# A fetched row's second operand moved to PSUM, with a new order of the pass over the experts

## The chip, the core and the metric

The kernel runs on one NeuronCore of a Trainium2 chip. Its engines run side by side, each through its own queue in order: PE (TensorE, matrix products), DVE (VectorE), ACT (ScalarE), POOL (GpSimd), and SP, which here only issues DMA transfers. Data lies in HBM, in SBUF (128 partitions) and in PSUM, 8 banks of 512 float32 per partition, into which PE writes its products. The metric is device microseconds (us) of one execution, lower is better.

## What is computed

One block of a diffusion backbone over 1024 tokens of width 1024: a state-space scan and long convolutions side by side, an output projection, and then PEER: per token 8 heads choose 16 experts each out of 16384, an expert being a row of `peer_u` and a row of `peer_v`. Only this last part is changed:

```python
def block(hb):
    q = (hb @ wq).reshape(PEER_BLOCK, PEER_HEADS, 2, PEER_DKEY // 2)
    s = jnp.einsum('thsd,snd->thsn', q, subkeys).astype(jnp.float32)
    s1, i1 = lax.top_k(s[:, :, 0], PEER_TOPK)
    s2, i2 = lax.top_k(s[:, :, 1], PEER_TOPK)
    ...
    idx = e1 * PEER_KEYS + e2
    gate = jax.nn.softmax(sc, axis=-1).astype(hb.dtype)
    u_sel = u_tab[idx]
    v_sel = v_tab[idx]
    act = jax.nn.gelu(jnp.einsum('td,thkd->thk', hb, u_sel), approximate=False) * gate
    return jnp.einsum('thk,thkd->td', act, v_sel)
```

Then follow the residual `h + g2 * peer` and a last RMS norm.

## The kernel before

The 1024 tokens are 8 blocks of 128, treated in two ways at the same time.

**Dense tokens**, blocks 0 to 4 (ND = 5, 640 tokens): their products with all 16384 experts, in 128 tiles of 128 experts, are made on PE, and the gates (zero where an expert isn't chosen) are multiplied in. Every float32 factor is split into a high part (ACT, a copy) and a low part (a subtraction on DVE or POOL), and a product is three matmuls: high by high, high by low, low by high.

- `score` (L1650): gelu of the dense tokens' products with a tile of `peer_u`. Tile `x_raw` is loaded (512 KB), split into `x_uh`, `x_ul`; 48 matmuls (8 x 3 x two halves of 320 tokens, L1665) go to `x_s`, two PSUM banks (SN = 2); one Gelu of 640 on ACT makes `x_a` (L1668).
- `up` (L1671): takes `x_a`, from `score` or, for tiles 0 to 47 (NE = 48), from memory (`d_A`), where they were put ahead of time; multiplies the gates `x_g` (DVE, L1684) and splits the result into `x_ah`, `x_al` (AB = 5 buffers each).
- `load_v` (L1631): half a tile of `peer_v`, 128 x 512, 256 KB; `x_vr` (VR = 2 raw buffers) is split into `x_vh` (ACT, L1638) and `x_vl` (POOL, L1639), VB = 4 buffers; `ahead_v` keeps VA = 3 ready.
- `down` (L1698): 15 matmuls (5 blocks x 3, L1712) of one A tile and one V tile into five PSUM banks `x_acc` at once (6 buffers); after the fourth tile of a group (SC = 4), DVE adds the five banks to the output `x_o` (L1719).

**The other three blocks**: `gathered` (L1563) fetches for each token its 128 rows of `peer_u` and 128 of `peer_v`, by indirect DMA from POOL's queue (L1556): one instruction fetches one row for each of 128 tokens, 512 KB, into one of the `rows` buffers (8 in the pass, 4 before it). For `peer_u`, DVE multiplies the fetched tile by the block's own rows `e_f` and sums (L1572); for `peer_v`, DVE adds it times a weight to an accumulator, also a tile named `e_f` (L1583). Both `e_f` lie in SBUF and share one buffer (EF = 1). 3 x 256 = 768 such tiles are fetched. `finish` (L1587) ends a block.

**The order.** `peer` (L1779) finds the chosen experts (`Route`) and spreads the gates; beside this run the first fetched rows and the 48 tiles computed ahead. Then `run` (L1754) passes over the 128 tiles in 32 groups of four: the first half of a group's output, tile by tile, then the up steps of the next group between the down steps of the second half, with `share` fetched rows after each step. Groups 0 to 11 hold the tiles computed ahead, groups 12 to 31 compute theirs. `last_half` ends the pass. A gather isn't put ahead of the last POOL split (`pace`). The order of each engine's queue is written out before the run by a scheduler that works from the program's order, what is ready, and buffers; it may put a later matmul ahead of one that would wait.

Of the kernel before, what the change touches and what calls it, by code (L numbers as in the profile page):

```python
# [21 lines left out]
D = 1024  # L22
# [9 lines left out]
class Kern:  # L32
# [11 lines left out]
    def pool(self, name, bufs=1, right=False, **kw):  # L44
        """a pool whose tiles wait for what stood on their own bytes alone"""
        return self.tc.tile_pool(name=name, bufs=bufs, side="right" if right else "left", reuse_waits="tile", **kw)

    def split(self, src, hi, lo, pool=False):
        """hi + lo == src, both exact in the tensor engine's one-pass float32."""
        self.nc.scalar.activation(hi, src, AF.Copy)  # L50
        (self.nc.gpsimd if pool else self.nc.vector).tensor_sub(lo, src, hi.bitcast(F32))  # L51

    def rstd(self, pool, ssum, n, shape, name):
        """1 / sqrt(ssum / n + eps)"""
# [7 lines left out]
    # ---------------------------------------------------------------- modulation  # L62
# [15 lines left out]
    def mod_sum(self, wp, s, j):  # L78
        """256 columns of the modulation for x (j = 0) or the context (j = 1), to be summed over the partitions"""
# [13 lines left out]
    def mod_norm1(self, ps, wp, j):  # L93
        """shift and scale of the first norm, features on the partitions, by 256 features"""
# [16 lines left out]
    def mod_rows(self, wp):  # L111
        """g1, sh2, norm2 * (1 + sc2), g2 as rows, to memory"""
# [18 lines left out]
    def row(self, pool, j, name):  # L131
        """row j of rows on all partitions"""
# [10 lines left out]
    # ---------------------------------------------------------------- x -> xT  # L143
# [5 lines left out]
    def normalize(self, wk, xs, xns, sq):  # L149
        """rows over their root mean square"""  # L150
# [8 lines left out]
    def xT(self, ps, wk, xns, b0, j, ks=range(8)):  # L159
        """transposes, modulates and splits blocks of tokens of x (j = 0) or the context (j = 1)"""  # L160
# [12 lines left out]
    # ---------------------------------------------------------------- in-projection  # L173
    def step(self, n):
        """goes on with the work beside"""
# [17 lines left out]
    def mm3_feat(self, outs, hi, lo, ks=range(8)):  # L193
        """outs: [(psum, 1 for the context, token offset, n)]; out[f, t] = sum_d w[d, f] x[t, d]"""
# [11 lines left out]
    def first_slab(self, ps, wp, wk, xs, mod, slab):  # L206
        """modulates x and takes it through the first slab's products as the modulation comes in"""
# [17 lines left out]
    def conv(self, acc, p, n, w, b, taps):  # L225
        """acc[:, t] = b + sum_j w[j] p[:, t + j - taps // 2], zero outside"""
# [11 lines left out]
    def to_tokens(self, ps, stage, acc, n):  # L238
        """stage[t, block, f] = acc[f, block * 128 + t]"""
# [96 lines left out]
    def softplus(self, x, tmp):  # L336
        """max(x, 0) + log1p(exp(-|x|)); log1p(e) = 2 atanh(e / (2 + e)); tmp: three scratches"""
# [92 lines left out]
class Ssd:  # L430
    """bidirectional chunked state-space scan; the context's states are carried in"""
# [65 lines left out]
    def advance(self, new, old, x, b, c, d):  # L497
        """new = old * exp(total) + sum_s B[s] (x w)[s]"""
# [17 lines left out]
    def states(self):  # L516
        """the states left of each chunk in the backward direction, to memory; the first forward state"""
# [36 lines left out]
    def load_cum(self, n):  # L554
        """the running sums of four heads, both directions, on all partitions"""
# [7 lines left out]
    def run(self):  # L563
        """all chunks, by groups of four heads: the first steps of a group go along with the last of the one before"""
# [25 lines left out]
    def first(self, c, g, loaded):  # L590
        """the weights between the tokens of a chunk before C B, and the inputs times their steps"""
# [31 lines left out]
    def second(self, c, g, loaded, made):  # L623
        """what a group of heads gives"""
# [28 lines left out]
    def done(self, c, loaded):  # L653
        """the state goes on; the chunk's output, normalized"""
# [18 lines left out]
class Hyena:  # L673
    """Long convolutions as products with DFT matrices, 2048 points for 1024 tokens.

    t = 128 n1 + n2 and k = k1 + 16 k2: a butterfly over n1 (on the vector engines) leaves the real and
    imaginary parts of k1 = 0..8, and a matrix over n2 for each k1 (on the tensor engine) gives the
    spectrum. Pair 0 holds the real sequences k1 = 0 and k1 = 8; the frequency 1024 takes the place of
    the imaginary part of frequency 0. The way back is the transpose. The work goes by slabs of W
    channels."""  # L680
# [13 lines left out]
    def tiles(self, p):  # L694
        """the four matrices of a pair: (out 0 of in 0, out 0 of in 1, out 1 of in 0, out 1 of in 1)"""
# [8 lines left out]
    def sin(self, x, r):  # L704
        """sin(x) in place, reduced to [-pi, pi] first"""
# [13 lines left out]
    def mlp(self):  # L719
        """the hidden layers of the filters' network; the last one's high parts, and below them its low parts"""  # L720
# [33 lines left out]
    def butterfly(self, u):  # L754
        """yields A = (real part, minus the imaginary part) of the sums over n1, pair by pair"""
# [122 lines left out]
    def filters(self):  # L878
        """the spectra of the two-sided filters (the biases with them), to memory"""
# [69 lines left out]
    def colmajor(self, dst, src, q):  # L949
        """dst[(w r), block] = rows of src in the grid's column-major order"""  # L950
# [359 lines left out]
ND = 5  # L1310
# [646 lines left out]
```

## Time and profile before

| | us |
|---|---|
| median of 3 runs | 4568.08 (4556.21 to 4576.03) |
| profiled execution, first to last instruction (its span) | 4564.0 |
| first fetched row's DVE instruction | 1994 |
| first matmul of a down step | 2774.6 |
| last instruction that computes (x_o, L1610) begins | 4552.3 |

A row of the profile's groups reads: line, engine, operation, output and inputs by the program's names, shapes, count | time in which at least one was running, mean of one in ns | idle time of the engine just before them, and who ended it. A row of a view of waits: who waited, for whom, total us, times, longest. A row of the windows view gives a stretch and the busy time of each engine in it with the count of instructions, then the granted PE clock, the busy share of the DMA engines and what they moved.

### The profile page before, as it was taken

The numbers are of one execution on the slowest core, as the hardware profiler recorded it, in microseconds if no ns is written. First come the engines' busy times: TensorE is split into PE (matmuls) and PEld (weight loads), VectorE is DVE, ScalarE is ACT, GpSimd is POOL, SyncE is SP. The second block draws the span as 40 slices with busy tenths as digits, with TensorE's granted clock in tenths as the row PEclk, the third lists the DMA queues.
The fourth block names the chain that finished last, engine by engine and source line by source line (L and its number), as shares of the span: only waits on it lengthen the run. The fifth ranks groups of instructions, "written<-read, shape, count | busy, mean of one in ns | idle before, by whom it ended". The sixth has DMA issues, their size and how long they took to land. (4 is left out here: it accounts for less than half of the span.)

```text
span 4564.0 us, 60591 instructions
## 1 busy us (share of the span) xinstructions
PE 3884.8 (85%) x21449; PEld 3372.0 (74%) x21449; DVE 3808.3 (83%) x6917; ACT 1325.5 (29%) x2292; POOL 2849.2 (62%) x2155
## 2 busy tenths in 40 slices
PE   5998998997876986888898877777989999998896
PEld 4776776786765875687898876655878888787784
DVE  5766888557999896699999995888798888888898
ACT  3323332234342221232225673111212222222221
POOL 2333434447777563065539895676787877788786
PEclk8999999998888998899999998889999999999998
DMA  6332333567644446456536447888798888888987
GB/s 202 99 114 99 111 124 107 162 200 232 192 159 137 145 135 178 157 209 237 185 139 212 170 164 267 290 294 290 263 314 309 303 308 307 273 299 295 317 298 242
DMA packets 509680, 974.13 MB, mean 213 GB/s; under 512 B 33772, under 2 KB 291232, under 8 KB 506433
## 3 DMA queue, kind: packets, MB, share of 16 engines
q1 hardware_dynamic: 395616, 557.25, 37.4%
q0 software_dynamic: 110880, 405.98, 25.3%
q10 hardware_dynamic: 2880, 7.03, 0.4%
q8 instruction: 169, 2.77, 0.2%
q14 instruction: 135, 1.10, 0.1%
HBM read 823.20 MB, written 146.95 MB: 213 GB/s over the span
## 5 line engine op out<-in xcount | busy, mean ns | idle before, releaser
L1556 POOL DMA_INDIRECT rows<-in_peer_u_dram,ids x384 | 524.5, 1366 | 222.4 <-DVE rows L1572 60.3
L1583 DVE SCALAR_TENSOR_TENSOR e_f<-rows,e_a,e_f 128x1024 f32<-128x1024 f32 x381 | 584.8, 1535 | 27.3 <-DMA rows<-in_peer_v_dram,ids 20.3
L1712 PE MATMUL x_acc<-x_vl,x_ah 128*128 128x512 f32 x1280 | 535.7, 418 | 84.4 <-POOL x_vl L1639 84.1
L1572 DVE SCALAR_TENSOR_TENSOR rows<-rows,e_f 128x1024 f32<-128x1024 f32 x384 | 576.4, 1528 | 27.7 <-DMA rows<-in_peer_u_dram,ids 21.9
L1556 POOL DMA_INDIRECT rows<-in_peer_v_dram,ids x384 | 499.6, 1301 | 121.3 <-issue 72.7
L1712 PE MATMUL x_acc<-x_vh,x_ah 128*128 128x512 f32 x1280 | 421.2, 416 | 123.4 <-ACT x_vh L1638 89.3
L1712 PE MATMUL x_acc<-x_vh,x_al 128*128 128x512 f32 x1280 | 519.7, 409 | 0.0
L1665 PE MATMUL x_s<-fTh,x_uh 128*128 128x320 f32 x2048 | 485.3, 316 | 22.6 <-ACT x_a L1668 20.7
L1665 PE MATMUL x_s<-fTh,x_ul 128*128 128x320 f32 x2048 | 486.6, 315 | 11.0 <-DVE x_ul L1628 10.9
L1665 PE MATMUL x_s<-fTl,x_uh 128*128 128x320 f32 x2048 | 483.6, 315 | 0.0
L1639 POOL TENSOR_TENSOR x_vl<-x_vr,x_vh 128x512 fp32r<-128x512 f32 x256 | 372.5, 1458 | 166.3 <-ACT x_vh L1638 151.9
L1712 PEld LDWEIGHTS x_acc<-x_vh,x_ah 128*128 128x128 f32 x1280 | 249.0, 199 | 191.5 <-ACT x_vh L1638 99.3
L1665 PEld LDWEIGHTS x_s<-fTh,x_uh 128*128 128x128 f32 x2048 | 355.7, 193 | 37.1 <-ACT x_a L1668 25.8
L1712 PEld LDWEIGHTS x_acc<-x_vl,x_ah 128*128 128x128 f32 x1280 | 256.8, 201 | 163.3 <-POOL x_vl L1639 112.0
L1665 PEld LDWEIGHTS x_s<-fTh,x_ul 128*128 128x128 f32 x2048 | 354.1, 193 | 16.4 <-DVE x_ul L1628 12.5
L1665 PEld LDWEIGHTS x_s<-fTl,x_uh 128*128 128x128 f32 x2048 | 353.6, 193 | 3.4
L1712 PEld LDWEIGHTS x_acc<-x_vh,x_al 128*128 128x128 f32 x1280 | 256.0, 200 | 52.5
L1638 ACT ACTIVATE x_vh<-x_vr 128x512 fp32r<-128x512 f32 x256 | 158.1, 625 | 466.0 <-DMA x_vr<-in_peer_v_dram 447.2
L1627 ACT ACTIVATE x_uh<-x_raw 128x1024 fp32r<-128x1024 f32 x128 | 135.3, 1057 | 492.1 <-PE x_s L1665 401.2
L1628 POOL TENSOR_TENSOR x_ul<-x_raw,x_uh 128x1024 fp32r<-128x1024 f32 x57 | 145.4, 2551 | 207.2 <-ACT x_uh L1627 205.2
L199 PE MATMUL mm<-xl,whi 128*128 128x512 f32 (+1 forms) x784 | 267.2, 412 | 7.2 <-DVE xl L51 7.2
L199 PE MATMUL mm<-xh,whi 128*128 128x512 f32 (+1 forms) x784 | 265.5, 413 | 7.8 <-DVE acc L235 4.1
(400 smaller groups left out, 9489.4 us busy)
## 6 DMA issues: line engine op xcount, KB each, us to landing
x_raw<-in_peer_uT_dram SPq DMA_DIRECT2D x128, 512.0 KB
x_vr<-in_peer_v_dram SPq DMA_DIRECT2D x256, 256.0 KB
d_G<-r_st SPq DMA_DIRECT2D x20, 2048.0 KB
x_g<-d_G SPq DMA_DIRECT2D x32, 1280.0 KB
wraw<-in_w_mod_dram SPq DMA_DIRECT2D x32, 1024.0 KB
wraw<-in_w_in_dram SPq DMA_DIRECT2D x24, 1024.0 KB
wk_w<-d_WK SPq DMA_DIRECT2D x24, 1024.0 KB
d_kr<-h_k SPq DMA_DIRECT2D x32, 512.0 KB
```

Source lines behind the costliest of these rows:

```text
L199: nc.tensor.matmul(p, w[:, k], x[j][:, k, t0:t0 + n], start=(k == 0 and q == 0), stop=(k == 7 and q == 2))
L1556: nc.gpsimd.indirect_dma_start(out=r, out_offset=None, in_=table, in_offset=bass.IndirectOffsetOnAxis(ap=ids[:, j:j + 1], axis=0))
L1572: nc.vector.scalar_tensor_tensor(r, r, 1.0, f, op0=ALU.mult, op1=ALU.mult, accum_out=d[:, j:j + 1])
L1583: nc.vector.scalar_tensor_tensor(acc, r, a[:, j:j + 1], acc, op0=ALU.mult, op1=ALU.add)
L1627: nc.scalar.activation(hi, raw, AF.Copy)
L1628: self.pace = (nc.vector if self.turn('u', UR if self.n < NE else UP) else nc.gpsimd).tensor_sub(lo, raw, hi.bitcast(F32)).ins
L1638: nc.scalar.activation(hi, raw, AF.Copy)
L1639: self.pace = nc.gpsimd.tensor_sub(lo, raw, hi.bitcast(F32)).ins
L1665: nc.tensor.matmul(s[:, m, :SW], w[:, k], x[:, k, m * SW:(m + 1) * SW], start=(k == 0 and q == 0), stop=(k == 7 and q == 2))
L1712: self.K.nc.tensor.matmul(self.p[b], a[x][:, bs], v[w], start=(m == 0 and q == 0), stop=(m == SC - 1 and q == 2))
```

## The change

The operand of the fetched rows goes to PSUM: the block's rows are loaded to a `rows` buffer, six rows before the block ahead of it ends, and copied by ACT to a tile `e_p` of two PSUM banks; the accumulator is a tile of the same name. The two banks are taken from `x_s`, now one bank for half of the tokens, two in turn (in routing as well as in the pass), and from `x_acc`: a down step is now one block of tokens, with all four tiles of a group in one bank, 12 matmuls, four banks in turn. So a half of the output needs four V tiles at once; one more fits (VB = 5, VA = 1), and the other three of the next half are asked for in the half's last step. A group has ten down steps, and the next group's four up steps come before steps 2, 5, 7 and 8 (UPS). The 48 tiles computed ahead are now the first one or two of each group (AHEAD): of a group's up steps, the one at step 2 is always loaded, that at step 5 for even groups, and those at 7 and 8 are computed. The residual of a fetched block works on the gate's buffer, since the accumulator lies in PSUM. AB goes from 5 to 8, the row buffers from 8 to 7. All docstrings are taken out (left out here; so lines have other numbers afterwards).

```diff
+    def load_ef(self, b):
+        f = self.row()
+        self.K.nc.sync.dma_start(f, self.K.T["f"][b * 128:(b + 1) * 128, :])
+        return f
...
-            f = gp.tile([128, D], F32, name="e_f", bufs=EF)
-            nc.sync.dma_start(f, K.T["f"][b * 128:(b + 1) * 128, :])
+            if b == ND:
+                self.ef = self.load_ef(b)
+            f = self.gps.tile([128, D], F32, name="e_p", bufs=1)
+            nc.scalar.activation(f, self.ef, AF.Copy)
             for j in range(128):
                 r = self.gather(K.i["peer_u"], ids, j)
                 nc.vector.scalar_tensor_tensor(r, r, 1.0, f, op0=ALU.mult, op1=ALU.mult, accum_out=d[:, j:j + 1])
...
-            acc = gp.tile([128, D], F32, name="e_f", bufs=EF)
+            acc = self.gps.tile([128, D], F32, name="e_p", bufs=1)
             for j in range(128):
                 r = self.gather(K.i["peer_v"], ids, j)
+                if j == 122 and b + 1 < NB:
+                    self.ef = self.load_ef(b + 1)
...
-        self.residual(self.K.nc.vector, acc, h, g)
-        self.norm(b, acc, h, fin)
+        V.tensor_mul(g, g, acc)
+        V.tensor_add(g, g, h)
+        self.norm(b, g, h, fin)
...
-            self.K.nc.sync.dma_start(raw, self.K.i["peer_uT"][self.nu].rearrange("p k e -> p (k e)"))
+            self.K.nc.sync.dma_start(raw, self.K.i["peer_uT"][U_ORDER[self.nu]].rearrange("p k e -> p (k e)"))
...
-        s = ps.tile([128, SN, 512], F32, name="x_s", bufs=self.sbufs)
-        for k in range(8):
-            for q, (w, x) in enumerate(((uh, fh), (uh, fl), (ul, fh))):
-                for m in range(SN):
-                    nc.tensor.matmul(s[:, m, :SW], w[:, k], x[:, k, m * SW:(m + 1) * SW],
-                                     start=(k == 0 and q == 0), stop=(k == 7 and q == 2))
         a = wk.tile([128, TD], F32, name="x_a", bufs=XA)
-        nc.scalar.activation(a.rearrange("p (m w) -> p m w", w=SW), s[:, :, :SW], AF.Gelu)
+        for m in range(SN):
+            ms = slice(m * SW, (m + 1) * SW)
+            s = ps.tile([128, 512], F32, name="x_s", bufs=2)
+            for k in range(8):
+                for q, (w, x) in enumerate(((uh, fh), (uh, fl), (ul, fh))):
+                    nc.tensor.matmul(s[:, :SW], w[:, k], x[:, k, ms], start=(k == 0 and q == 0), stop=(k == 7 and q == 2))
+            nc.scalar.activation(a[:, ms], s[:, :SW], AF.Gelu)
...
-        if e < NE:
+        if e in AHEAD:
             a = wk.tile([128, TD], F32, name="x_a", bufs=XA)
-            nc.sync.dma_start(a, K.T["A"][e])
+            nc.sync.dma_start(a, K.T["A"][AHEAD.index(e)])
...
-    def down(self, g, half, m):
-        v = self.V.pop((g, half, m))
-        self.ahead_v(VA)
-        if m == 0:
-            self.p = [self.ps.tile([128, 512], F32, name="x_acc", bufs=6) for _ in range(ND)]
-        for b in range(ND):
-            self.product(b, m, self.A[g][m], v)
-            if m == SC - 1:
-                self.add(g, half, b)
...
+    def down(self, g, half, b):
+        if b == 0:
+            self.v = [self.V.pop((g, half, m)) for m in range(SC)]
+        p = self.ps.tile([128, 512], F32, name="x_acc", bufs=PA)
         bs = slice(b * 128, (b + 1) * 128)
+        for m in range(SC):
+            a, v = self.A[g][m], self.v[m]
+            for q, (x, w) in enumerate(((0, 0), (0, 1), (1, 0))):
+                self.K.nc.tensor.matmul(p, a[x][:, bs], v[w], start=(m == 0 and q == 0), stop=(m == SC - 1 and q == 2))
+        self.ahead_v(VA if b < ND - 1 else SC)
         dst = self.acc[:, b, half * 512:(half + 1) * 512]
...
-        share = (left - LASTG) / (2 * SC * (n - 1) + 2 * (NT - NE))
+        share = (left - LASTG) / (2 * ND * (n - 1) + ND + 2.6 * (NT - NE))
         self.A, self.V, self.nv = {}, {}, 0
-        self.ahead_v(VA)
-        for g in range(n + 1):
-            if g:
-                for m in range(SC):
-                    self.down(g - 1, 0, m)
-                    self.some(share if g < n else (LASTG + 1.01) / SC)
-            for m in range(SC):
-                if g < n:
-                    self.up(g, m)
-                    if SC * g + m >= NE:
-                        self.some(2 * share)
-                    if g:
-                        self.down(g - 1, 1, m)
-                        self.some(share)
+        self.ahead_v(SC)
+        for m in range(SC):
+            self.up(0, m)
+            self.some(2.6 * share if m not in AHEAD else 0)
+        for g in range(n):
+            units = [(h, b) for h in range(2 if g < n - 1 else 1) for b in range(ND)]
+            for u, (h, b) in enumerate(units):
+                if g < n - 1 and u in UPS:
+                    e = SC * (g + 1) + UPS.index(u)
+                    self.up(g + 1, UPS.index(u))
+                    if e not in AHEAD:
+                        self.some(2.6 * share)
+                self.down(g, h, b)
+                self.some(share)
             if g:
...
+                self.A.pop(g - 1, None)
+        for _ in self.rows:
+            pass
         self.last_half()
...
-AB = 5
-VB = 4
+AB = 8
+VB = 5
...
-VA = 3
-RB2 = 8
+VA = 1
+RB2 = 7
+PA = 4
+UPS = (2, 5, 7, 8)
...
+AHEAD = [4 * g + m for g in range(32) for m in range(2 - g % 2)]
+U_ORDER = AHEAD + [e for e in range(128) if e not in AHEAD]
...
+                X.gps = late.enter_context(K.pool("xgp", space=PSUM))
                 peer(K, X, R)
```

More of the change, by code (lines that the diff above doesn't have):

```diff
@@ L1587, in finish @@
     def finish(self, b, acc):
+        V = self.K.nc.vector
         h, g, fin = self.row(), self.row(), self.row()
@@ L1696, in ahead_v @@
             self.nv += 1
-    def down(self, g, half, m):
-        v = self.V.pop((g, half, m))
-        self.ahead_v(VA)
-        if m == 0:
-            self.p = [self.ps.tile([128, 512], F32, name="x_acc", bufs=6) for _ in range(ND)]
-        for b in range(ND):
-            self.product(b, m, self.A[g][m], v)
-            if m == SC - 1:
-                self.add(g, half, b)
-    def product(self, b, m, a, v):
-        bs = slice(b * 128, (b + 1) * 128)
-        for q, (x, w) in enumerate(((0, 0), (0, 1), (1, 0))):
-            self.K.nc.tensor.matmul(self.p[b], a[x][:, bs], v[w], start=(m == 0 and q == 0), stop=(m == SC - 1 and q == 2))
-    def add(self, g, half, b):
+    def down(self, g, half, b):
+        if b == 0:
+            self.v = [self.V.pop((g, half, m)) for m in range(SC)]
+        p = self.ps.tile([128, 512], F32, name="x_acc", bufs=PA)
+        bs = slice(b * 128, (b + 1) * 128)
+        for m in range(SC):
[3 more added lines that the diff above has]
+        self.ahead_v(VA if b < ND - 1 else SC)
         dst = self.acc[:, b, half * 512:(half + 1) * 512]
         if g == 0:
-            self.K.nc.vector.tensor_copy(dst, self.p[b])
+            self.K.nc.vector.tensor_copy(dst, p)
         else:
-            self.K.nc.vector.tensor_add(dst, dst, self.p[b])
+            self.K.nc.vector.tensor_add(dst, dst, p)
     def last_half(self):
         g = NT // SC - 1
-        self.ahead_v(SC)
-        v = [self.V.pop((g, 1, m)) for m in range(SC)]
         gate, fin = self.row(), self.row()
@@ L1736, in last_half @@
                 else:
-                    self.p[b] = self.ps.tile([128, 512], F32, name="x_acc", bufs=6)
-                    for m in range(SC):
-                        self.product(b, m, self.A[g][m], v[m])
-                    self.add(g, 1, b)
+                    self.down(g, 1, b)
                 self.residual(self.K.nc.vector if half else self.K.nc.gpsimd, self.acc[:, b, hs], self.h[b][:, hs], gate[:, hs])
@@ L1754, in run @@
     def run(self, pool, wk, ps):
-        self.wk, self.ps, self.sbufs = wk, ps, 1
+        self.wk, self.ps = wk, ps
         self.acc = pool.tile([128, ND, D], F32, name="x_o")
@@ L1781, in peer @@
     with K.pool("rx") as xk, K.pool("rp", space=PSUM) as ps:
-        X.wk, X.ps, X.sbufs = xk, ps, 2
+        X.wk, X.ps = xk, ps
         X.rp, X.rb = xk, RB
@@ L1846, in back @@
         X = Experts(K, R, gp, xu)
-        with K.pool("rm", right=True) as mid:
-            R.tables(mid)
-            out_proj(K, R)
-            peer(K, X, R)
-        X.pour(RB2)
+        with ExitStack() as late:
+            with K.pool("rm", right=True) as mid:
+                R.tables(mid)
+                out_proj(K, R)
+                X.gps = late.enter_context(K.pool("xgp", space=PSUM))
+                peer(K, X, R)
+            X.pour(RB2)
 def block(ctx, tc, i, o):
```

1 line of the change is left out of this document (removed).

## Prediction

> **What bounds the kernel now.** I read the windows view first, cut where the fetched rows begin, where the pass over all experts begins (2765 us) and where its computed tiles begin.
>
> ```profile
> core 0: us, PE busy (x) PEld busy (x) DVE busy (x) ACT busy (x) POOL busy (x), PEclk, DMA share, GB/s
> 1930.00:2765.00 835.00, 714.18 (x5007) 697.50 (x5007) 807.05 (x2265) 355.25 (x689) 569.03 (x322) 0.93 0.52 188
> 2765.00:3255.00 490.00, 384.83 (x1499) 298.30 (x1500) 397.58 (x386) 97.17 (x151) 339.02 (x249) 0.90 0.85 285
> 3255.00:4490.00 1235.00, 1125.36 (x6014) 1000.46 (x6014) 1078.15 (x1155) 279.20 (x396) 984.83 (x684) 0.96 0.87 299
> 4490.00:4564.00 74.00, 34.62 (x123) 25.07 (x121) 56.75 (x58) 14.68 (x27) 42.35 (x29) 0.76 0.65 228
> 2680.00:2700.00 20.00, 12.06 (x86) 10.76 (x85) 20.00 (x28) 13.19 (x35) 20.00 (x12) 0.91 0.34 145
> 2720.00:2740.00 20.00, 14.76 (x119) 14.10 (x120) 16.43 (x37) 17.12 (x44) 20.00 (x16) 1.00 0.41 172
> ```
>
> Three stretches with three limits. In 1930 to 2765 ("routing") DVE is busy 807 of 835 us, only at its end POOL takes over (20 of 20 us). In 2765 to 3255 ("light": groups 0 to 11, whose up steps only load tiles) nothing is full: PE 79%, DVE 81%, DMA share 0.85. In 3255 to 4490 ("heavy": groups 12 to 31, all computed) PE has 91%, DVE 87%, POOL 80%, DMA 0.87: several engines near full, coupled.
>
> A busy PE counts overlapping matmuls, so I price PE by start to start, from the timeline:
>
> ```profile
> 3004.52 0.39 PE L1712 MATMUL x_acc<-x_vh,x_al 128*128 128x512 f32 x1
> 3004.75 0.39 PE L1712 MATMUL x_acc<-x_vl,x_ah 128*128 128x512 f32 x1
> 3601.01 0.46 PE L1665 MATMUL x_s<-fTh,x_uh 128*128 128x320 f32 x2
> 3601.30 0.46 PE L1665 MATMUL x_s<-fTl,x_uh 128*128 128x320 f32 x2
> ```
>
> A down matmul takes 0.23 us, a score matmul 0.29 / 2 = 0.146. A group has 120 down matmuls (27.6 us), a computed tile 48 score matmuls (7.0 us). The light stretch issues 12 x 27.6 = 331 of 490 us (68%), the heavy one 20 x 27.6 + 80 x 7.0 = 1112 of 1235 (90%; the cut is not exact to a tile). PE stands still for about a third of the light stretch.
>
> The DVE rows, from the tile views and from the groups by line (the first of these of 1930 to 2765, the next two of 2765 to 4490):
>
> ```profile
> L1572 DVE SCALAR_TENSOR_TENSOR rows<-rows,e_f x384: 1169/1214/5798, 1994.1 to 4228.2; 128x1024 f32<-128x1024 f32 x192
> L1583 DVE SCALAR_TENSOR_TENSOR e_f<-rows,e_a,e_f x381: 1270/1285/4300, 2876.4 to 4522.9; 128x1024 f32<-128x1024 f32 x191
> L1719 DVE TENSOR_TENSOR x_o<-x_o,x_acc x310: 669/677/691, 2829.0 to 4541.1; 128x512 f32<-128x512 f32 x155
> L1603 DVE TENSOR_TENSOR x_o<-x_o,rows x5: 677/679/1170, 4536.7 to 4546.5; 128x512 f32<-128x512 f32 x5
> L1572 DVE SCALAR_TENSOR_TENSOR rows<-rows,e_f 128x1024 f32<-128x1024 f32 x106 | 178.2, 1684 | 6.1 <-DMA rows<-in_peer_u_dram,ids 6.1
> L1583 DVE SCALAR_TENSOR_TENSOR e_f<-rows,e_a,e_f 128x1024 f32<-128x1024 f32 x365 | 560.7, 1536 | 26.9 <-DMA rows<-in_peer_v_dram,ids 20.3
> L1572 DVE SCALAR_TENSOR_TENSOR rows<-rows,e_f 128x1024 f32<-128x1024 f32 x278 | 398.2, 1468 | 21.6 <-DMA rows<-in_peer_u_dram,ids 15.8 <-DMA e_f<-d_f 5.3 <-issue 0.3
> ```
>
> Three numbers after "x384:" are minimum, median, maximum in ns. Instructions with both inputs in SBUF (the first two and L1603) have tails far over their medians; the 310 adds with one input in PSUM (x_acc) run 669 to 691, with no tail.
>
> **Operand in PSUM.** What goes is the tail. Mean less median: 106 x (1684 - 1214) = 50 us in routing; 365 x (1536 - 1285) + 278 x (1468 - 1214) = 92 + 71 = 163 us after it. What the operand itself costs: the L1572 form is shown with PSUM nowhere, and no row shows DVE writing PSUM as L1583 will. Nearest: at 512 wide, 677 with PSUM, 679 without: no difference, the value I take. Ends: two such adds for 1024 (2 x 677 = 1354, +0.14 us on 768 rows, +108 us of DVE) and L1572's minimum 1169 (-0.05, -38 us).
>
> [...]
>
> In routing DVE is the limit, so its 50 us count nearly whole, but POOL closes the stretch, and POOL work that no longer meets a row can meet another two-input instruction. I take **-30** (0 to -50).
>
> New per block of tokens: one ACT copy of 1024 into PSUM.
>
> ```profile
> L1668 ACT ACTIVATE x_a<-x_s x128: 680/687/712, 1944.4 to 4485.7; 128x640 f32<-128x640 f32 x128
> L1627 ACT ACTIVATE x_uh<-x_raw 128x1024 fp32r<-128x1024 f32 x128 | 135.3, 1057 | 492.1 <-PE x_s L1665 401.2
> DVE rows L1572 <- DMA e_f<-d_f: 5.3, 1, 5.3
> ACT x_ah L50 <- PE x_acc L1712: 198.6, 51, 12.5
> ACT x_vh L1638 <- DMA x_vr<-in_peer_v_dram: 423.0, 115, 21.6
> PE x_acc L1712 <- ACT x_vh L1638: 83.3, 24, 8.6
> PE x_acc L1712 <- POOL x_vl L1639: 78.1, 52, 4.8
> PE x_s L1665 <- ACT x_a L1668: 20.7, 13, 2.7
> PE x_acc L1712 <- DVE x_o L1719: 17.5, 13, 3.5
> ```
>
> Three copies of about 1.06 us replace a 5.3 us wait for a load, since f is now loaded six rows before the block ends: nothing in the sum. The load holds one row buffer of seven (eight before); rows were late only 20.3 + 15.8 us in 1725, so nothing for that either, with +20 as its other end.
>
> **Up step in halves.** 24 matmuls for 320 tokens, Gelu, again: the same 48 matmuls, 128 more ACT instructions, each under the 0.69 us of a whole tile's Gelu, on an engine busy 97 + 279 = 376 of 1725 us. A second bank removes the 20.7 us wait of x_s for x_a. In routing the scores lose two of four banks; DVE, not PE, sets that stretch, so nothing (+15 if ACT's late Gelus show).
>
> **Down step by block.** Still 120 matmuls a group and ten adds; one bank per block, four in turn, so an add (0.68 us) has three rounds of 12 x 0.23 = 2.8 us: most of the 17.5 us wait for x_o goes. AB 8 holds two groups' A tiles: the 198.6 us that ACT stood before x_ah with its queue (x_vh behind it) goes. The price is that a half needs four V tiles at once, and only one of the next four fits beforehand (VB 5). That is the rival below; in the forecast I leave today's 161 us of x_acc waiting for x_vh and x_vl in place, because waits on other tiles can be filled: four banks let blocks 1 to 3 start with tiles that are there, and scores lie between.
>
> **Spreading.** Matmuls, rows and bytes stay: 32 x 27.6 + 80 x 7.0 = 1443 us of issue. Only the evenness changes: 44 to 45 us of PE a group instead of 28 then 56, and about 20 rows instead of 13 then 26. At the heavy stretch's 90% the whole would take 1443 / 0.90 = 1603 us instead of 1725 (-122). Against that stands DMA:
>
> ```profile
> DMA packets 230962, 509.50 MB, mean 295 GB/s; under 512 B 16991, under 2 KB 98911, under 8 KB 230858
> ```
>
> 509.5 MB at the heavy stretch's 299 GB/s take 1704 us (-21). 299 is not a ceiling: share 0.87 there, so 299 / 0.87 = 344 at share 1 by proportion, and 0.90 would give 309. DVE falls by 163 to about 1313 us and no longer resists. I take the middle, **1660** us (307 GB/s, PE 87%): -65.
>
> **Sum**, against the profiled 4564.0 us: -30 - 65 = 4469. The end (4490 to 4564) keeps its work. The median of the runs is 4568.08, 4 us more, so the forecast is **4473 us**. With routing from -50 to 0 and the pass from 1625 to 1700 us its own range is 4420 to 4530.
>
> **Rivals.**
>
> *A: V tiles in a burst (slower).* Rows for the refill:
>
> ```profile
> L1638 ACT ACTIVATE x_vh<-x_vr x256: 612/629/637, 2765.4 to 4529.7; 128x512 fp32r<-128x512 f32 x128
> L1639 POOL TENSOR_TENSOR x_vl<-x_vr,x_vh x256: 1260/1317/2322, 2767.9 to 4532.1; 128x512 fp32r<-128x512 f32 x128
> SPq L1635 <- POOL x_vl L1639: 902.7, 232, 12.5
> 3021.12 1.09 SPq L1635 DMA_DIRECT2D x_vr<-in_peer_v_dram  x1
> 3027.76 0.63 ACT L1638 ACTIVATE x_vh<-x_vr 128x512 fp32r<-128x512 f32 x1 [8.30 <-DMA x_vr<-in_peer_v_dram]
> ```
>
> From the start of a half's last block: tile 1 of the next half may be split when the old tile 0 is done (0.7 us), is split at 0.7 + 0.6 + 1.3 = 2.6, and only then has the fourth raw tile a buffer (VR 2; SP's queue already waits 902.7 us on x_vl). Its load takes up to 6.6 us (3021.12 to 3027.76), I take 5; splits 1.9: ready at 9.5. PE, in order, wants it at 2.8 + 9 x 0.23 = 4.9: 4.6 us of stall. POOL waits at x_vl too, and the gathers behind it: seven row buffers cover some 7 x 2.6 us. A score lies in only 16 of 64 boundaries, so 48 x 4.6 = 221 us, in place of today's 161: +60, with all gain of spreading gone, -30 in routing: **4598**. It decides from a stall of (161 + 30) / 48 = 4.0 us per boundary that PE's order, written out before the run, doesn't fill; at the full 6.6 us of load it would be 80 us more. For it: loads are late 423 us already. Against: today's order does put scores between down matmuls. 0.17.
>
> *B: DMA stays at 299 GB/s:* 1704 us: **4517**. For it: light and heavy differ little (285, 299). 0.18.
>
> *C: PE keeps 93%,* since DVE no longer delays x_o and x_al: 1443 / 0.93 = 1552, routing -45: **4350**. It needs 328 GB/s, share 0.95, above any stretch shown. 0.12.
>
> *D: the operand change gives little.* PSUM rows at 1354, or the blocked time moves to x_a, x_al and x_ul, and spreading gives its DMA-bound 21 at best: **4550**. 0.08.
> [...]
>
> **Chances.** Forecast 0.45, A 0.17, B 0.18, C 0.12, D 0.08. A change under 0.5% (23 us) can't be told from none: runs of this kernel spread over 20 us. Faster: forecast, B, C, less a little of B: 0.72. Same: D and that little, 0.10. Slower: A, 0.18 with rounding. The range leaves out about half of A above and half of C below: 4375 to 4600.
>
> **What would show it.** Operand: L1572 and L1583 with maxima near their medians and means of about 1.21 and 1.29; over 1.35, D. Routing: the pass starts some 30 us earlier. Spreading: windows from there are even, PE near 87%, DMA 305 GB/s or more; 299 is B. Down step: x_acc's wait for x_vh and x_vl at or under 161 us; over 220 is A, with POOL x_vl waiting for x_vh and gathers late. Wrong altogether would be a new wait on PE for the copy into e_p or for x_s banks in routing.

## The result and the profile after

The kernel after takes **4363.57 us** (median of 4 runs, 4355.85 to 4378.38) against 4569.63 us (4 runs) for the kernel before: ratio 0.9551, 95% interval 0.9517 to 0.9585. It gained 206 us; the forecast of 4473 us had 95, and its range of 4375 to 4600 ends just above the result. The profiled execution has a span of 4366.7 us (before: 4564.0).

The windows view of the kernel after, cut at its own stages (columns as in the prediction):

```profile
1930.00:2725.00 795.00, 699.57 (x5015) 685.94 (x5015) 763.17 (x2281) 364.37 (x744) 544.32 (x325) 0.94 0.56 201
2725.00:4290.00 1565.00, 1459.55 (x7491) 1275.61 (x7492) 1325.21 (x1533) 388.17 (x629) 1086.19 (x926) 0.97 0.92 324
4290.00:4367.00 77.00, 35.05 (x143) 27.11 (x141) 57.84 (x59) 14.79 (x28) 39.32 (x32) 0.75 0.67 238
```

Routing went from 835 to 795 us (-40), the pass from 1725 to 1565 (-160), the end from 74 to 77: together the 197 us between the two spans. In the pass PE is now busy 93% of the time, and DMA moves 324 GB/s at share 0.92, where no long stretch of before had more than 299 at 0.87. The slices of the page show that light and heavy stretches are gone:

```profile
PEclk8999999899888899789999998999999999999998
DMA  6332333366764444646745644889999999999997
GB/s 203 99 120 94 110 121 127 114 211 176 239 184 162 133 130 126 186 157 239 255 146 187 237 172 193 276 296 321 338 337 321 332 334 329 327 330 342 337 321 259
```

The tile view of the fetched rows, after, and for the gathers also before (minimum/median/maximum in ns):

```profile
L1556 POOL DMA_INDIRECT rows<-in_peer_u_dram,ids x384: 934/942/4247, 1987.6 to 4033.3; - x192
L1580 DVE SCALAR_TENSOR_TENSOR rows<-rows,e_p x384: 1164/1209/1223, 1998.8 to 4045.8; 128x1024 f32<-128x1024 f32 x192
L1556 POOL DMA_INDIRECT rows<-in_peer_v_dram,ids x384: 934/942/1839, 2792.9 to 4313.0; - x192
L1593 DVE SCALAR_TENSOR_TENSOR e_p<-rows,e_a,e_p x381: 1274/1290/1293, 2807.9 to 4320.8; 128x1024 f32<-128x1024 f32 x191
L1577 ACT ACTIVATE e_p<-rows x3: 1028/1029/1030, 1939.6 to 3749.3; 128x1024 f32<-128x1024 f32 x3
L1591 DVE TENSOR_SCALAR e_p<-rows,e_a x3: 1275/1287/1287, 2805.9 to 4049.0; 128x1024 f32<-128x1024 f32 x3
```

```profile
L1556 POOL DMA_INDIRECT rows<-in_peer_u_dram,ids x384: 934/1358/3049, 1982.9 to 4220.2; - x192
L1556 POOL DMA_INDIRECT rows<-in_peer_v_dram,ids x384: 935/1181/2158, 2866.6 to 4512.0; - x192
```

Both forms of the row instruction keep their medians (1214 to 1209, 1285 to 1290) and lose their tails: the maxima fall from 5798 and 4300 ns to 1223 and 1293. What the prediction did not have is in the gathers: POOL's median falls from 1358 and 1181 to 942 ns. The waits of the pass, after:

```profile
ACT x_vh L1650 <- DMA x_vr<-in_peer_v_dram: 314.6, 91, 14.8
ACT x_ah L50 <- PE x_acc L1719: 70.9, 19, 8.3
PE x_acc L1719 <- ACT x_vh L1650: 56.7, 24, 8.8
PE x_acc L1719 <- POOL x_vl L1651: 18.5, 20, 2.9
PE x_acc L1719 <- DVE x_o L1725: 12.4, 7, 3.2
PE x_s L1679 <- ACT x_a L1680: 5.1, 5, 3.2
```

PE's waits for V tiles fell from 83.3 + 78.1 = 161 us to 75, ACT's wait for a free A buffer from 198.6 to 71 us.

### The profile page after: what moved, and what is told of

Read it like the earlier page. It is cut to its first block, busy times and chain, and to the rows that moved or that the text cites. A ratio compares the mean times of both kernels' runs of the same rounds, so it can differ in the third digit from the quotient of the medians.

```text
span 4366.7 us, 60771 instructions
## 1 busy us (share of the span) xinstructions
PE 3831.1 (88%) x21449; PEld 3348.9 (77%) x21449; DVE 3611.4 (83%) x6917; ACT 1344.1 (31%) x2423; POOL 2580.7 (59%) x2155
## 5 line engine op out<-in xcount | busy, mean ns | idle before, releaser
L1679 PE MATMUL x_s<-fTh,x_uh 128*128 128x320 f32 x2048 | 644.3, 315 | 8.2 <-ACT x_a L1680 8.2
L1679 PE MATMUL x_s<-fTh,x_ul 128*128 128x320 f32 x2048 | 641.9, 314 | 6.8 <-DVE x_ul L1640 6.8
L1679 PE MATMUL x_s<-fTl,x_uh 128*128 128x320 f32 x2048 | 642.6, 314 | 0.0
L1556 POOL DMA_INDIRECT rows<-in_peer_u_dram,ids x384 | 413.1, 1076 | 204.6 <-DVE rows L1580 72.6
L1593 DVE SCALAR_TENSOR_TENSOR e_p<-rows,e_a,e_p 128x1024 f32<-128x1024 f32 x381 | 489.7, 1285 | 35.2 <-DMA rows<-in_peer_v_dram,ids 26.5
L1580 DVE SCALAR_TENSOR_TENSOR rows<-rows,e_p 128x1024 f32<-128x1024 f32 x384 | 455.8, 1210 | 39.4 <-DMA rows<-in_peer_u_dram,ids 36.0
L1556 POOL DMA_INDIRECT rows<-in_peer_v_dram,ids x384 | 401.7, 1046 | 135.9 <-issue 68.6
L1679 PEld LDWEIGHTS x_s<-fTh,x_ul 128*128 128x128 f32 x2048 | 391.5, 191 | 16.4 <-DVE x_ul L1640 7.9
L1679 PEld LDWEIGHTS x_s<-fTl,x_uh 128*128 128x128 f32 x2048 | 392.6, 192 | 9.2
L199 PE MATMUL mm<-xh,wlo 128*128 128x512 f32 (+1 forms) x784 | 263.8, 411 | 0.4 <-POOL wlo L51 0.4
```

What stands on the lines that cost most here:

```text
L199: nc.tensor.matmul(p, w[:, k], x[j][:, k, t0:t0 + n], start=(k == 0 and q == 0), stop=(k == 7 and q == 2))
L1556: nc.gpsimd.indirect_dma_start(out=r, out_offset=None, in_=table, in_offset=bass.IndirectOffsetOnAxis(ap=ids[:, j:j + 1], axis=0))
L1580: nc.vector.scalar_tensor_tensor(r, r, 1.0, f, op0=ALU.mult, op1=ALU.mult, accum_out=d[:, j:j + 1])
L1593: nc.vector.scalar_tensor_tensor(acc, r, a[:, j:j + 1], acc, op0=ALU.mult, op1=ALU.add)
L1679: nc.tensor.matmul(s[:, :SW], w[:, k], x[:, k, ms], start=(k == 0 and q == 0), stop=(k == 7 and q == 2))
```

## The experiments

The kernel before was run beside every group of runs (medians 4561 to 4577 us); a ratio is to those, with its 95% interval. Differences to the kernel after (4364) compare medians of different groups.

### The change taken apart

**order_alone**: the new order and the A and V buffers only; operand in SBUF (where only six row buffers fit), tiles 0 to 47 ahead.

```diff
-            f = self.gps.tile([128, D], F32, name="e_p", bufs=1)
+            f = gp.tile([128, D], F32, name="e_p", bufs=1)
...
-            acc = self.gps.tile([128, D], F32, name="e_p", bufs=1)
+            acc = gp.tile([128, D], F32, name="e_p", bufs=1)
...
-RB2 = 7
+RB2 = 6
...
-AHEAD = [4 * g + m for g in range(32) for m in range(2 - g % 2)]
+AHEAD = list(range(NE))
```

> The kernel after with the operand in SBUF, six row buffers and the tiles computed ahead as tiles 0 to 47: the new order of the down step, the halves and the eight A tiles alone. If spreading pays only once the fetched rows are fast (it gave -83 us with the operand in PSUM and +27 us on the kernel before): within 30 us of the 4590 that the same kernel gave with the tiles spread, near or below the kernel before with some help from the A tiles. If spreading pays with this order whatever the rows cost: 4640 to 4680.

Measured: 4612 us, 1.0095 (1.0066 to 1.0123).

**operand_sbuf6**: the same, tiles spread (without the last edit above).

> The changed kernel with the operand and the accumulator of the fetched rows in SBUF again (and one row buffer less, since they need its place); all else as changed. If the operand is the source: the tails of the row instructions return (means 1.47 and 1.54 us) and the time rises by 100 us or more over the same kernel with six row buffers, to 4470 or more. If evenness or the order of the down step is: 30 to 50 us more than that one, from routing alone.

Measured: 4590 us, 1.0052 (1.0035 to 1.0069).

**rows6**: operand in PSUM, six row buffers (RB2 = 6 is the only edit).

> The changed kernel with six row buffers, the control for the run with the operand in SBUF. Rows were late only some 57 us in the pass: 4365 to 4400 us by all theories.

Measured: 4417 us, 0.9674 (0.9657 to 0.9690), above the 4365 to 4400 expected.

These last two differ in the place of the operand alone; SP's queue has the same order in both, the others nearly. The tile view, a window and a wait in that window of operand_sbuf6, then of rows6:

```profile
L1556 POOL DMA_INDIRECT rows<-in_peer_u_dram,ids x384: 935/1328/4187, 1986.4 to 4249.8; - x192
L1580 DVE SCALAR_TENSOR_TENSOR rows<-rows,e_p x384: 1170/1215/6308, 1997.6 to 4263.4; 128x1024 f32<-128x1024 f32 x192
L1593 DVE SCALAR_TENSOR_TENSOR e_p<-rows,e_a,e_p x381: 1267/1285/3954, 2871.7 to 4552.1; 128x1024 f32<-128x1024 f32 x191
L51 DVE TENSOR_TENSOR x_al<-x_a,x_ah x128: 799/816/3365, 2797.9 to 4455.5; 128x640 fp32r<-128x640 f32 x128
```

```profile
2900.00:4200.00 1300.00, 1167.87 (x5897) 1012.95 (x5896) 1111.25 (x1196) 303.50 (x491) 1007.47 (x699) 0.96 0.87 296
PE x_acc L1719 <- POOL x_vl L1651: 53.9, 44, 3.9
```

```profile
L1556 POOL DMA_INDIRECT rows<-in_peer_u_dram,ids x384: 932/940/4243, 1987.3 to 4105.5; - x192
L1580 DVE SCALAR_TENSOR_TENSOR rows<-rows,e_p x384: 1165/1209/1223, 1998.5 to 4118.1; 128x1024 f32<-128x1024 f32 x192
L1593 DVE SCALAR_TENSOR_TENSOR e_p<-rows,e_a,e_p x381: 1272/1289/1292, 2805.6 to 4369.4; 128x1024 f32<-128x1024 f32 x191
L51 DVE TENSOR_TENSOR x_al<-x_a,x_ah x128: 809/818/4741, 2736.2 to 4289.9; 128x640 fp32r<-128x640 f32 x128
```

```profile
2900.00:4200.00 1300.00, 1222.05 (x6292) 1070.06 (x6291) 1074.48 (x1288) 320.58 (x521) 885.13 (x744) 0.97 0.91 317
PE x_acc L1719 <- POOL x_vl L1651: 10.9, 16, 1.6
```

With the operand in SBUF the tails and the long gathers are back, and DMA moves 296 GB/s, as before the change. With it in PSUM the first x_al comes 62 us earlier (2736 for 2798), DMA moves 317 GB/s, and the whole is 173 us shorter. PE's wait for x_vl, which POOL makes behind the gathers, falls from 53.9 to 10.9 us, while its wait for x_vh (ACT's) stays: 61.1 and 64.1 us in the same stretch. The rows of rows6 also tell what the seventh buffer is worth: its last fetched row begins at 4369.4, 79 us after its last x_al; in the kernel after it is 26 us (4320.8, with the last x_al at 4295.1). Nearly all of the 53 us between the two kernels is rows left over at the end.

**no_spread**: the kernel after, with tiles 0 to 47 ahead. **spread_alone**: the kernel before, with the spread list and the order of `peer_uT` that goes with it.

```diff
-AHEAD = [4 * g + m for g in range(32) for m in range(2 - g % 2)]
+AHEAD = list(range(NE))
```

> The changed kernel with the tiles computed ahead put back into groups 0 to 11. If evenness is the source: back up by 100 us or more, 4460 to 4500, with a light and a heavy stretch again. If the operand is: at most 40 us more than the change, 4365 to 4400.

> Before with its 48 tiles computed ahead spread over all groups, nothing else. If the gain of the pass (1725 to 1565 us) is the evenness, this gives most of it: 4430 to 4460 us. If DVE's and POOL's blocked time is what held the pass, its heavy stretch's limits now hold everywhere and this stays near before: 4530 to 4590. The down step by block taken as the source says the same as the latter.

Measured: no_spread 4447 us, 0.9742 (0.9726 to 0.9758); spread_alone 4591 us, 1.0054 (1.0037 to 1.0070). Spreading is worth 83 us once the operand stands in PSUM, costs some 25 us in the kernel before, and is worth 22 us with the new order and the operand in SBUF (order_alone to operand_sbuf6). The 83 us lie between what the two sides had expected (at most 40, or 100 and more).

So, one edit after the other: order and buffers, with six row buffers, 4570 to 4612 (+42); spreading 4590 (-22); operand in PSUM 4417 (-173); the row buffer for which the operand's SBUF makes room 4364 (-53).

### Whose time the operand gives back

In the pass the operand returns time on two engines: tails on DVE, and 0.30 us of each gather on POOL (mean 1.36 before, 1.05 after, from the records of the pass). Two runs put time back on one engine each. Their added instructions also make the scheduler write out another order, as in share_a and share_b below, where another order alone moved the time by 8 to 13 us.

**dve_pad**: DVE copies 128 columns of e_p after each row of the pass. **pool_pad**: a POOL memset before each gather. **pool_pad2**: the same memset on the row buffer itself.

```diff
+                if self.rb == RB2:
+                    nc.vector.tensor_copy(gp.tile([128, 128], F32, name="e_x", bufs=1), f[:, 0:128])
...
+        if self.rb == RB2:
+            nc.gpsimd.memset(r[:, 0:240], 0.0)
```

> The changed kernel with one more DVE instruction behind each fetched row's in the pass: a copy of 128 columns from PSUM to a scratch nobody reads, about 0.29 us by the copy of 160 columns (326 ns), some 186 us of DVE in the pass, a little more than the 170 us of tails that the change took off DVE there; without a second SBUF input, so POOL is not held. If the pass was held by DVE's time, it comes back by 100 us or more: 4465 to 4550. If what counted was POOL's time (gathers 1.36 to 1.05 us) or the gathers' start, under 50 us: 4365 to 4415.

> The changed kernel with one more POOL instruction ahead of each gather of the pass: a memset of 240 columns to a scratch nobody reads, about 0.3 us by the memset of 128 columns (205 ns), some 190 us of POOL, about the 205 us that the gathers lost. If POOL's time is what the change freed: 4450 to 4550. If DVE's is: under 40 us, 4365 to 4405.

> The kernel after, with a POOL memset of 240 columns (about 300 ns, as the memsets of the run before measured) on the row buffer itself ahead of each gather of the pass: some 662 x 0.3 = 198 us of POOL work, about what its gathers got shorter by (1.355 to 1.051 us each). If DVE's row stream is what the PSUM operand freed and POOL's shorter gathers only came with it, POOL (1086 of 1565 us busy) still has room: +0 to +35 us against the 4364 of the kernel after. If POOL's shorter gathers are half of the gain or more: +70 us or more, with rows falling behind and a longer stretch after the last up step.

The tile views of the added instructions of dve_pad, pool_pad and pool_pad2, in this order:

```profile
L1597 DVE COPY e_x<-e_p x384: 274/291/294, 2800.2 to 4436.7; 128x128 f32<-128x128 f32 x192
L1582 DVE COPY e_x<-e_p x278: 273/280/291, 2656.3 to 4153.9; 128x128 f32<-128x128 f32 x139
```

```profile
L1556 POOL MEMSET e_y<- x662: 289/298/702, 1786.6 to 2380.3; 128x240 f32 x166
```

```profile
L1556 POOL MEMSET rows<- x662: 288/313/329, 2647.8 to 4385.4; 128x240 f32 x166
```

dve_pad took 4469 us, 0.9783 (0.9740 to 0.9825): +105 for 662 x 0.287 = 190 us of DVE; its gathers kept medians of 940 and 939 ns (942 in the kernel after), so the copies did not lengthen them. pool_pad took 4389 us (+25), but tells nothing of the pass: its memsets wait for no row buffer and all ran between 1787 and 2380 us, ahead of the pass, as their row shows. pool_pad2 took 4444 us, 0.9738 (0.9687 to 0.9790): +81 for 662 x 0.313 = 207 us of POOL, which contradicts what I had expected of a POOL with room (0 to +35). Both engines matter: in these two runs a microsecond put on DVE costs 0.55, one on POOL 0.39. They cost it in different places. In dve_pad the rows fall behind, as its tile views show: 131 us from the last x_al to the last row, 26 in the kernel after. These 105 us more at the end are as much as the whole difference; from the first x_al to the last it is only 16 us longer than the kernel after. In pool_pad2 this stretch is 73 us longer, and in operand_sbuf6 it is 104 us longer than in rows6. The x_al row of dve_pad with its last rows, then the x_al row of pool_pad2:

```profile
L51 DVE TENSOR_TENSOR x_al<-x_a,x_ah x128: 807/816/4946, 2730.5 to 4304.8; 128x640 fp32r<-128x640 f32 x128
L1595 DVE SCALAR_TENSOR_TENSOR e_p<-rows,e_a,e_p x381: 1273/1290/1292, 2800.5 to 4435.4; 128x1024 f32<-128x1024 f32 x191
```

```profile
L51 DVE TENSOR_TENSOR x_al<-x_a,x_ah x128: 804/817/4756, 2732.4 to 4363.9; 128x640 fp32r<-128x640 f32 x128
```

In pool_pad2 the V splits behind the gathers are late: its waits between 2900 and 4200 us, where the kernel after has 44.3 us for x_vh and 15.1 for x_vl.

```profile
PE x_acc L1721 <- ACT x_vh L1652: 88.1, 20, 7.9
PE x_acc L1721 <- POOL x_vl L1653: 27.6, 15, 5.5
```

### The A tiles

**ab7_rows8**: seven A tiles and eight row buffers. **ab7**: seven A tiles only. **ab7_vb6**: seven A tiles and a sixth V buffer. **share_a**, **share_b**: only the number of rows per step, and with it the written order, changes slightly.

```diff
-AB = 8
+AB = 7
...
-RB2 = 7
+RB2 = 8
...
-VB = 5
-VA = 1
+VB = 6
+VA = 2
...
-LASTG = -8
+LASTG = -4
```

> The changed kernel with eight row buffers and seven of A tiles. If the row stream is held by its buffers (gathers waited 110 us for rows that DVE was yet to use): 20 to 50 us faster, 4315 to 4345. If DMA is full or the A tiles' last buffer counts as much: within 15 us, or slower by up to 40 as x_ah waits for x_acc again.

> The kernel after with seven buffers for A tiles instead of eight, and seven row buffers as there. If ACT standing before x_ah for a free A buffer, with x_vh queued behind it, made the run with seven A tiles and eight row buffers 81 us longer: +60 to +95 us against 4364 here too, with ACT's wait of x_ah for x_acc near 135 us and PE's wait for x_vh near 130 us. If it was the eighth row buffer (more gathers in flight beside the loads): within 15 us of 4364, and those waits near 65 and 45.

> The kernel after with seven A tiles, and the room of the eighth given to a sixth V buffer (VA 2). If x_vh is late because ACT is held at x_ah, a further V buffer doesn't help much: +45 to +90 us against 4364, like seven A tiles alone. If x_vh is late because a half's four V tiles come in a burst with one buffer to spare (rival A of the prediction): two to spare take back most of it, within 20 us of 4364 or below.

> The kernel after with LASTG -4 instead of -8: a few rows fewer (about 4 in 650) are placed ahead of the pass's end, nothing else changes but the order that the scheduler writes out. If the order alone moves the time by tens of us, this run and the next lie 20 us or more from 4364 to either side, and the +37 and +48 us of the runs with seven A tiles show nothing. If such changes of order are worth little: both within 15 us of 4364.

> The same with LASTG -12, a few rows more placed ahead. Expected as for share_a: within 15 us of 4364 if the order alone is worth little, 20 us or more away if it is not.

| | us | ratio, interval | to after |
|---|---|---|---|
| ab7_rows8 | 4445 | 0.9722 (0.9694 to 0.9750) | +81 |
| ab7 | 4401 | 0.9631 (0.9602 to 0.9659) | +37 |
| ab7_vb6 | 4412 | 0.9647 (0.9620 to 0.9674) | +48 |
| share_a | 4372 | 0.9575 (0.9542 to 0.9607) | +8 |
| share_b | 4376 | 0.9574 (0.9550 to 0.9598) | +13 |

Waits between 2900 and 4200 us, of the kernel after, ab7 and ab7_rows8:

```profile
ACT x_ah L50 <- PE x_acc L1719: 64.6, 17, 8.3
PE x_acc L1719 <- ACT x_vh L1650: 44.3, 20, 5.0
```

```profile
ACT x_ah L50 <- PE x_acc L1719: 91.9, 18, 11.9
PE x_acc L1719 <- ACT x_vh L1650: 58.7, 16, 8.0
```

```profile
ACT x_ah L50 <- PE x_acc L1719: 138.5, 25, 9.6
PE x_acc L1719 <- ACT x_vh L1650: 133.0, 24, 10.6
```

In these three runs PE waits longer for x_vh the longer ACT stands before x_ah; both go through ACT's queue in order. That this delay is the cause isn't shown: ACT's wait for the loads of x_vr grows as well (252.9, 282.2 and 382.3 us), and gate_layout below has 83.3 us before x_ah and only 4.7 for x_vh. The profile of ab7 is also that of its fastest execution, 4376 us. The expectation of ab7 (+60 to +95) was missed: one A tile is worth 37 us. The other 44 of ab7_rows8, itself slower than either of its expectations (-50 to +40), came with the eighth row buffer. Why a row buffer more should cost isn't settled; the written order differs too, though share_a and share_b show that another order alone moves the time by 8 to 13 us. A sixth V buffer took nothing back: with seven A tiles, V tiles are not short of buffers.

### What the transfers allow

**gates_once**: x_g is loaded for the first group only and used for all; 31 gate loads (40.6 MB) are left out, so tiles from the second group on get the first group's gates.

**gate_layout**: the gates lie in memory so that an x_g load reads one piece of 10 KB per partition instead of 20 of 512 bytes; routing writes pieces of 512 bytes instead of 16 KB. **before_layout**: the same in the kernel before. **gate_pitch**: pieces as in the kernel after, addresses changed by padding.

```diff
-            self.g4 = self.gates(e)
+            if g == 0:
+                self.g4 = self.gates(e)
...
-    T["G"] = dr.tile([TD // GT, 128, 128, GT], F32, name="d_G")
+    T["G"] = dr.tile([128, 128 // SC, TD // GT, SC, GT], F32, name="d_G")
...
-            nc.sync.dma_start(K.T["G"][b * (128 // GT) + q], st)
+            nc.sync.dma_start(K.T["G"][:, :, b * (128 // GT) + q], st.rearrange("p (g m) t -> p g m t", m=SC))
...
-        nc.sync.dma_start(t, K.T["G"].rearrange("q p e t -> p q e t")[:, :, e:e + SC, :])
+        nc.sync.dma_start(t, K.T["G"][:, e // SC])
...
-    T["G"] = dr.tile([TD // GT, 128, 128, GT], F32, name="d_G")
+    T["G"] = dr.tile([TD // GT, 128, 132, GT], F32, name="d_G")
```

> The changed kernel with the gates of group 0 used for all groups, which leaves 31 loads of x_g out: 31 x 1.31 = 40.6 MB of the pass's 507. If the pass is now bound by DMA (324 GB/s, share 0.92): 125 us less at that rate, at least 70, so 4240 to 4295. If PE (93% busy) or the waits between engines hold it: at most 30 us, 4335 to 4365.

> The kernel after with the gates in memory laid out so that a load of x_g in the pass reads 10 KB in one piece for each partition instead of 20 pieces of 512 bytes; the stores in routing now write pieces of 512 bytes instead of 16 KB. Same bytes, same order on every engine. If DMA transfers bound the pass (share 0.92): some 80000 small packets leave it, at an estimated 34 ns each against 22 ns for the same bytes in large ones, 0.98 ms over 16 DMA engines, 61 us at most; 20 to 55 us faster than 4364, in the pass, and routing within 10 us of today since its DMA share is 0.56. If the queues on ACT, POOL and PE bound it and a load is late only by its place in the queue: within 12 us of 4364. If the small stores delay routing: the pass starts 10 us or more later.

> The kernel before, with nothing changed but the layout of the gates in memory that made the kernel after 74 us faster (same bytes, same order on every engine, large pieces in the pass). If the 299 GB/s of the kernel before was what DVE's slow rows and the waits for V tiles left to ask for, and not a limit of the transfers: 0 to -30 us against 4571. If DMA bound that pass as well: -55 to -75 us, as in the kernel after.

> The kernel after with the gates in memory as before, in pieces of 512 bytes, but with four unused tiles of padding behind each partition's 128, so that the pieces that are read stand 16.5 KB apart between partitions instead of 16 KB, and 2.06 MB between token groups instead of 2 MB. Same bytes, same pieces, same order. If the 76 us of the other layout came from the size of the pieces: within 12 us of 4364. If they came from where the pieces lie (distances that are powers of two): 40 to 76 us faster than 4364.

| | us | ratio, interval | difference |
|---|---|---|---|
| gates_once | 4245 | 0.9283 (0.9254 to 0.9312) | -118 to after |
| gate_layout | **4289** | 0.9384 (0.9358 to 0.9410) | -74 to after |
| gate_pitch | 4356 | 0.9524 (0.9499 to 0.9550) | -8 to after |
| before_layout | 4517 | 0.9898 (0.9875 to 0.9921) | -44 to before |

gates_once gained 118 us of the 125 that its 40.6 MB take at 324 GB/s, as expected of a pass bound by its transfers. The same 1300 us of the pass, by windows and by the DMA view, of the kernel after and then of gate_layout:

```profile
2900.00:4200.00 1300.00, 1224.40 (x6281) 1069.27 (x6280) 1116.34 (x1320) 324.21 (x523) 910.09 (x777) 0.97 0.93 330
```

```profile
DMA packets 194559, 429.40 MB, mean 330 GB/s; under 512 B 14293, under 2 KB 83413, under 8 KB 194471
q1 hardware_dynamic: 116012, 142.57, 33.6%
```

```profile
2900.00:4200.00 1300.00, 1257.95 (x6572) 1105.45 (x6571) 1179.09 (x1373) 339.70 (x549) 961.26 (x821) 0.99 0.94 344
```

```profile
DMA packets 135034, 447.70 MB, mean 344 GB/s; under 512 B 14985, under 2 KB 14985, under 8 KB 131613
q1 hardware_dynamic: 52048, 144.66, 30.7%
```

The waits of gate_layout in the same stretch:

```profile
ACT x_vh L1650 <- DMA x_vr<-in_peer_v_dram: 203.8, 84, 7.3
ACT x_ah L50 <- PE x_acc L1719: 83.3, 20, 10.9
PE x_acc L1719 <- ACT x_vh L1650: 4.7, 4, 1.5
```

Every engine has the order of the kernel after, and bytes are the same; q1, the queue with the gate loads, moves 144.66 MB in 30.7% of the engines' time where it took 33.6% for 142.57. ACT's wait for x_vr falls from 252.9 to 203.8 us, PE's wait for x_vh from 44.3 to 4.7. So late transfers were what PE still waited for. The gain is larger than expected (20 to 55 us, 61 at most; its 34 and 22 ns for 512 bytes are an estimate from the queues of the kernel after between 2725 and 4290 us, q0 with 337.24 MB in 58.4% of the engines' time and q1 with 168.26 MB in 33.0%): by share per byte the loads of q1 take some 43 us less of this stretch, and where the rest of the 74 us comes from isn't shown. gate_pitch, with the small pieces at other addresses, gives none of it beyond the spread. As far as this one padding shows, it is the size of the pieces. gate_layout is the fastest complete version, 6% under the kernel before.

The same windows of the kernel before and of before_layout:

```profile
2900.00:4200.00 1300.00, 1148.86 (x5752) 992.69 (x5751) 1117.63 (x1194) 285.91 (x413) 1001.62 (x701) 0.94 0.87 297
```

```profile
2900.00:4200.00 1300.00, 1171.40 (x5940) 1007.52 (x5941) 1155.00 (x1241) 295.83 (x427) 1045.65 (x724) 0.97 0.87 306
```

I had expected -30 at most, or -55 and more; -44 lies between. Transfers already cost the kernel before something, but at share 0.87 it goes from 297 to 306 GB/s only, which fits a pass that its rows held as well.

## Why the prediction was right or wrong

**Direction and reason: right.** The largest single step is the operand (-173 us), and it works as stated: the tails go, the operand itself costs nothing. 1209 against 1214 ns and 1290 against 1285 show no cost of the PSUM operand in these two instructions. Not priced were the three first v rows, 753 ns in SBUF and 1287 in PSUM, 1.6 us in all.

**Routing: nearly right.** -40 for a forecast of -30 (0 to -50), but partly by luck. The operand alone starts the pass 62 us earlier (operand_sbuf6 to rows6), more than the 50 us of tails that the prediction counted at most (in operand_sbuf6 they are 66 us: 109 rows with a mean of 1805 ns, 1202 in rows6). operand_sbuf6 enters the pass 22 us later than the kernel before (first matmul of a down step at 2796.8 for 2774.6), so the rest of the change, put at nothing, costs routing about that. The two errors nearly cancel.

**The pass: the failed step.** The prediction took "the middle, 1660 us", between a transfer-bound 1704 at 299 GB/s and PE's 1603 at the heavy stretch's 90%. It measured 1565. Both ends were readings of the old pass that the change itself moved. 299 GB/s was taken as close to what DMA gives, though the same paragraph worked out 344 at share 1; the new pass moves 324 and gate_layout 344 in its middle. And PE's 90% already held the tails on DVE and the long gathers on POOL. 1443 us of matmul issue in 1565 is 92%: rival C, whose 93% and 328 GB/s gave 4350, was 14 us off, and had 0.12 with the remark that it lay "above any stretch shown". Its number was right, its reason only in small part: it named DVE's delay of x_o and x_al, but PE's wait for x_o fell by 5 us and that for V tiles by 86. That no stretch shows a rate says little where what asks for the transfers is the thing that changes. (By the prediction's own terms its own range ends at 4543 us, 4568 - 25, and not at 4530.)

**POOL: missing.** The sum gave the operand's return to DVE only. By the prices of the two pads, DVE's return in the pass (605 rows x 0.25 us between operand_sbuf6 and rows6, by their records) and POOL's (612 gathers x 0.30) are worth 0.55 x 151 + 0.39 x 184 = 83 + 72 = 155 us; the pair differs by 173 - 62 = 111 us after routing. So the two don't simply add up. DVE's price is rows left over at the end, 105 us of them, and operand_sbuf6 has only 17 us more of these than rows6 (97 after its last x_al for 79). In between it loses 104 us and PE's wait for x_vl rises, as with POOL's pad, so POOL's share is not small; its size isn't settled. The traces show the two engines meet: before, each of the 144 row instructions that took over 1.3 times its form's median overlaps a two-input instruction on POOL, mostly x_vl; of the 310 x_o adds with one input in PSUM 100 overlap one and none is that long, and after, 334 of the 765 rows overlap one and none is. POOL's side: x_vl has means of 1.453 and 1.333 us in the pass before and after (1.489 and 1.351 between 2800 and 4250 us in operand_sbuf6 and rows6), and the gathers' medians are 1328 and 940 ns with the operand as the only difference. A little of the time moved to DVE instructions whose two inputs stay in SBUF: in the pass the mean of x_a went from 1153 to 1284 ns and that of x_al from 1092 to 1137, 22 us over 127 of each.

**V tiles: wrong both ways.** Rival A's burst didn't happen, and "today's 161 us ... in place" was too careful: the wait fell to 75 us. The prediction named ACT's 198.6 us before x_ah, with x_vh queued behind it, and gave its going no price. One of the eight A tiles proves to be worth 37 us. But with the operand in SBUF a shorter wait of ACT alone did little for PE: between 2900 and 4200 us it was 52 us in operand_sbuf6 (130 before), and PE waited 61 us for x_vh (65 before). What fell with the operand is the wait for POOL's x_vl. ab7_vb6 shows that, with seven A tiles, V buffers are not what is short.

**Spreading: right as a mechanism, wrong as a term of its own.** Windows are even (PE is busy 93 to 95% in each 300 us from 3000 to 4200), and it gives 83 us with fast rows; with the new order and slow rows it gives 22, and alone it costs some 25 us. The prediction priced it at half of 122 whatever the rows do.

**The row buffer: too cheap.** Nothing, at most +20, for one of eight. One of seven costs 53 us, for rows that remain after the last step. What the step from eight to seven costs has no clean run.

**Small terms:** the three copies on ACT (1.03 us each) and the halves (PE's wait of x_s for x_a fell from 20.7 to 5.1 us) are as predicted. That most of the wait for x_o would go was wrong (17.5 to 12.4 us), at a cost of a few us.

## What to carry to other kernels

When an edit frees several engines at once, don't carry over the old stage's rates (GB/s, PE's share) as bounds of the new one: first ask what they were waiting for, and give the case where they rise a real chance. When an instruction has long tails, look also at what runs beside it on another engine: here the medians of POOL's gathers went from 1358 and 1181 to 942 ns when DVE's rows lost theirs. When the transfers have become the bound, look at the size of the pieces before the number of bytes: a layout of one table gave 74 us here, with no instruction's order changed.

## What the hardware showed

- An indirect gather's own instruction on POOL takes 940 ns at the median when DVE's rows have one SBUF operand and 1328 when they have two (rows6, operand_sbuf6); what in the gather takes longer is not shown.
- With the 32 loads of x_g (1.31 MB each) in pieces of 10 KB instead of 512 bytes, the kernel took 4289 us instead of 4364 (gate_layout), at a DMA share of 0.94 between 2900 and 4200 us, 0.93 in the kernel after. Their queue q1 took 30.7% of the engines' time for 144.66 MB, where it took 33.6% for 142.57.
- DMA kept 344 GB/s over 1300 us at share 0.94 with gathers and loads mixed (gate_layout).
- A DVE instruction that still has two SBUF inputs, x_al, has its tail after the change as before it (median 820, maximum 5855 ns; before 818 and 3639):

```profile
L51 DVE TENSOR_TENSOR x_al<-x_a,x_ah x128: 809/820/5855, 2736.5 to 4295.1; 128x640 fp32r<-128x640 f32 x128
```
